# Full-height rotary matmul in attention scores, one round-robin burst for the in-chunk kernels of a block, and a planner class for 64-column matmuls

## The chip, the cores and the metric

The kernel runs on one core of a Trainium2 chip. The metric is the device time of one execution in microseconds. PE is TensorE (PEld is its weight load), DVE is VectorE, ACT is ScalarE, POOL is GpSimd and SP is SyncE, which issues most DMAs.

## What is computed

The program is a trunk of two layers over 256 latent tokens and 256 context tokens of width 1024, in float32. Each layer does a half-step SwiGLU FFN, then two token mixers on one normed input, then a second half-step FFN. All are wrapped in RMS norms with modulation from a conditioning vector. The two parts of the mixer that matter here:

```python
def mla_attend(q_n, q_r, k_n, k_r, v):
    s = jnp.einsum('bqhd,bkhd->bhqk', q_n, k_n) + jnp.einsum('bqhr,bkr->bhqk', q_r, k_r)
    p = jax.nn.softmax(s.astype(jnp.float32) * MLA_SCALE, axis=-1).astype(v.dtype)
    return jnp.einsum('bhqk,bkhd->bqhd', p, v)
```

There are 8 heads; a score has a part over 128 channels (q_n, k_n) and a rotary part over 64 channels (q_r, k_r). The other mixer is a bidirectional diagonal state-space layer (S5) of 64 groups of 16 channels with 64 complex states each:

```python
    xs_c = s5_scan(uc, a_bar, b_bar, reverse, None)
    xs_x = s5_scan(ux, a_bar, b_bar, reverse, s_ctx)
    y_x = y_x + s5_readout(xs_x, c_mat).reshape(B, L, S5_WIDTH)
```

In the last layer only the latent tokens are needed after the mixer.

## The kernel before

**Numbers.** Most products take three matmuls: an operand is split into a rounded part (hi) and a rest (lo), and hi·hi, hi·lo and lo·hi are added in one bank. Weights stream from DRAM as 256 KB pieces (`raw`), which ACT and DVE split into `whi` and `wlo`.

**The planner.** Instructions are not issued in the order of the text. `Recorder` records them all, each with a key (the time on the main path at which it was recorded, plus a shift for work that stands aside), and `schedule` (line 379) then simulates the engines and emits a list order; so every instruction of the trace has the emitter's line, L576, and is told apart by its tiles. A PE instruction has a mode (line 340): 1 for a stationary operand of at most 32 columns, 2 for all others. When the ready instruction with the least key is of another mode than the engine's present one, the planner first looks for ready ones of the present mode whose keys lie up to `TILE_PULL` = 12000 ns later (line 342). It charges `TILE` = 90 ns for a change into mode 2 only (line 498). Tiles of 512 columns come from a pool of `SLOTS` = 71 (line 27), shared by weights, activations and temporaries.

**Attention** (line 1311). A score (line 1359) is five matmuls into one bank for a 128-row block of queries and 512 or 256 keys: three for the 128 channels, then two for the rotary part. The rotary queries of a head are stacked as `st`: 64 partitions hold their hi, the other 64 their lo. The rotary keys stand twice, on both halves of the 128 partitions, as `krh` and `krl`. The fourth matmul takes all 128 rows, `st` by `krh`; the fifth takes only the 64 rows with the hi part, by `krl` (tiles `lo,qs` in the trace). There are 48 scores: 32 in layer 0 (16 by 512 keys and 16 by 256) and 16 in layer 1 (by 512).

**S5 build** (line 1599). This is done once per layer, beside the FFN ahead of the mixer, as recorded steps with keys pushed back by 15000 ns (layer 0) or 10000 ns (layer 1). For each of 8 blocks DVE makes `bz` (stationary columns, 32 for a pair of directions and group; one lasting tile for all blocks) and four readout tables `P` of 512 columns (two halves of the groups by two directions). A callback three steps after a half's second table records `kernels` (line 1668): 8 matmuls of 32 stationary columns by 128 moving ones (tiles `P,c`), four into one 32-partition group of the bank `kp`, then four into the next, and then the DMAs that store the tables. So a block has 16 matmuls in two calls; the profiler records two for each, 32 of a block and 512 in all. Afterwards `kout` copies the bank and the next tables follow.

**S5 run** (line 1734). This runs beside the mixer. For a block, 32 matmuls with 64 stationary columns (`uc,m1l`, 64 records) give the inputs; DVE rotates and scans; the states `X` are read out with 64-column matmuls in layer 0 (`X,pl` and `uc,tt`, 96 records of a block) and with 32-column ones in layer 1 (`pl,X` and `tt,uc`). Results go to DRAM and come back (`ys`) for the GLU that follows the attention output product.

**Others with 32 columns** are the modulation products (`aw,c`: a round-robin over the four 32-partition groups of a bank, line 791) and the norms' column sums (`tri,c`, `sq,c`).

Of the kernel before, what the change touches and what calls it, by code (L numbers as in the profile page):

```python
# [9 lines left out]
F32 = mybir.dt.float32  # L10
# [12 lines left out]
LEAD = 6  # L23
# [3 lines left out]
SLOTS, HALVES, ROWS, TRIS = 71, 8, 8, 4  # L27
# [45 lines left out]
class View:  # L73
    """A part of an on-chip tile, as strides over [128 partitions, columns]."""
# [55 lines left out]
    def extent(self):  # L130
        """The first partition, the last, and the columns as bits."""
        p, c = divmod(self.offset(), self.root.cols)
        key = c, self.arr.shape[1:], self.arr.strides[1:]
        if key not in MASKS:
            at = np.array([c])
            for n, st in zip(*key[1:]):
                at = (at[:, None] + st * np.arange(n if st else 1)).reshape(-1)
            m = 0
            for x in at.tolist():
                m |= 1 << x  # L140
            MASKS[key] = m
        return p, p + self.arr.shape[0], MASKS[key]
# [14 lines left out]
class Root:  # L157
    """A tile: lasting, or one of a tag's buffers from its first write to its last use."""
# [18 lines left out]
class Scratch:  # L177
    """A part of a DRAM tensor, with what tells it from parts that other instructions use."""
# [41 lines left out]
class Recorder:  # L220
    """Records instructions, then issues them in the order of a list schedule.

    An instruction waits for those that it depends on and for its buffers; each engine takes the one that was
    recorded for the earliest time among those that can run.
    """
# [18 lines left out]
    # ---------------------------------------------------------------- tiles  # L244
# [14 lines left out]
    # ---------------------------------------------------------------- priorities  # L259
    @contextmanager  # L260
    def aside(self, late, pace=0.0, lazy=False):
        """Work beside the main path, as if recorded some time later, and by and by.

        Lazy work is for an engine's idle time, up to the time at which its result is needed.
        """
# [8 lines left out]
    # ---------------------------------------------------------------- recording  # L274
    def cost(self, eng, method, a, kw):
        """Time on the engine, in ns."""
# [26 lines left out]
    def record(self, engine, method, a, kw):  # L303
# [35 lines left out]
        elif engine.code == "PE":  # L339
            op.mode = 1 if a[1].shape[-1] <= 32 else 2  # L340
# [37 lines left out]
    # ---------------------------------------------------------------- schedule  # L378
    def schedule(self):
# [12 lines left out]
        n = 0  # L392
# [35 lines left out]
        while left:  # L428
# [8 lines left out]
            for e in engines:  # L437
# [59 lines left out]
                if op.mode not in (0, mode[e]):  # L497
                    extra = self.TABLE if e == "ACT" else self.TILE if op.mode == 2 else 0
# [46 lines left out]
    def lacks(self, op):  # L545
        """A tile that the instruction is the first to use and that has to wait for a buffer, if there is one.

        A tile gets a buffer only if all that is still to come, in the order of the recording, then fits as well.
        """
# [29 lines left out]
class Trunk:  # L579
# [24 lines left out]
    # ---------------------------------------------------------------- storage  # L604
# [21 lines left out]
    # ---------------------------------------------------------------- fillers  # L626
    def add_filler(self, gen, interval, delay=0.0, late=0, pace=0.0, lazy=False):
        """A generator whose steps are recorded at intervals, with the priority of a later time.

        With a pace the intervals are that many times VectorE's work in a step.  # L630
        """
# [21 lines left out]
    # ---------------------------------------------------------------- weights  # L653
# [8 lines left out]
    def wget(self):  # L662
        """Loads and splits the weights that come next."""
# [14 lines left out]
    # ---------------------------------------------------------------- matmuls  # L678
# [20 lines left out]
    # ---------------------------------------------------------------- norms  # L699
    def part(self, t, h):  # L700
        """Half h of the tokens of a tile: 0 the context, 1 the latent ones, which an x-only tile holds alone."""
# [10 lines left out]
    def stat(self, r, q, n=1):  # L712
        """Adds a block's column sums to n regions of the statistics bank: 4 quadrants by 64 tokens."""
# [5 lines left out]
    def rsqrt(self, v, plain=False, wide=True, times=1.0, mask=None):  # L719
        """times/sqrt of [quadrant, token] rows: as they are, and with the tokens of other quadrants as zeros."""  # L720
# [28 lines left out]
    def rstd(self, r, width, n=1):  # L749
        """1/rms of the sums of squares in n regions from r on."""  # L750
# [4 lines left out]
    def spread(self, p, rows):  # L755
        """Rows of 64 tokens, one of each quadrant, to [128, 256 tokens] on every partition."""
# [8 lines left out]
    def close(self, l, s, i, h, y, src, fast, last=False):  # L765
        """Statistics of half h of block i of a branch's output: sums of src^2, y^2 and x y for y = G src."""
# [21 lines left out]
    # ---------------------------------------------------------------- modulation  # L788
    ADA_AHEAD = 4

    def ada_gen(self, units):
        """One step: one [128, 512] piece of ada_w for the two conditioning vectors."""
# [45 lines left out]
    def ada_first(self):  # L838
        """One step: a quarter of the channels of the two units that the first norm needs."""
# [24 lines left out]
    def ada_rows(self, units):  # L864
        """The same on the vector engine: one step gives 128 channels from their rows of the transposed ada_w."""
# [59 lines left out]
    # ---------------------------------------------------------------- FFN  # L925
    def lead(self, nrm, evac):
        """The first LEAD output blocks of a phase by pairs, one half of the tokens after the other."""
# [29 lines left out]
    def ffn(self, l, f, nrm, nxt):  # L957
        """nrm gives the normed input; nxt(y) makes the Norm that takes the output."""
# [58 lines left out]
    def gate_half(self, g, n):  # L1017
        """Makes the gated block j of half h of the tokens from a bank with both of its products."""
# [7 lines left out]
    def ffn_last(self, l, nrm):  # L1026
        """The last branch: its output has the tokens on partitions, where the norm has one scale per partition."""
# [75 lines left out]
    # ---------------------------------------------------------------- mixer  # L1103
# [197 lines left out]
    def rope(self, t):  # L1301
        """Axial rotation of [128 = two heads of 64, 256 x tokens], in place."""
# [8 lines left out]
    def attention(self, l, xo, cq, ckv, krh, krl):  # L1311
# [47 lines left out]
        def score(p, qs, kv, j, c, nk):  # L1359
            (qh, ql), st = qs[0][j], qs[1][j]  # L1360
            kh, kl = kv[0][j]
            a = slice(0, 64) if j == 0 else slice(64, 128)
# [5 lines left out]
            nc.tensor.matmul(p, st[a, c], krl[a, ks], start=False, stop=True)  # L1368
# [72 lines left out]
    # ---------------------------------------------------------------- S5  # L1441
    def cmul(self, ore, oim, are, aim, bre, bim, tmp):
        """Complex product of equal-shaped views; tmp: two scratch views; outputs may not alias inputs."""
# [8 lines left out]
    def s5_tables(self, l):  # L1452
        """Per-state tables: 192 columns; 0..63 (pair, dir) with (g2, n) on partitions, 64..191 (dir, g) with n twice."""
# [70 lines left out]
        # decay over eight steps  # L1524
# [5 lines left out]
        # unit phases 8, 16, 32, .. steps  # L1530
# [28 lines left out]
        # powers of the transition: 0..7 in the stacked columns, 1..8 in the pair columns  # L1559
# [39 lines left out]
    def s5_build(self, l):  # L1599
        """Per layer: chunk matrices to DRAM. Tensor-engine parts follow their operands by some steps."""  # L1600
# [6 lines left out]
        bz = self.s5c["bz"]  # L1607
# [21 lines left out]
        # rotation tables over the chunks  # L1629
# [16 lines left out]
        for b in range(NB):  # L1646
            stg = self.stg[l][b]
            pa, pb, pc = nxt
            # stacked b_bar in 32-column blocks of a pair, zero elsewhere
# [15 lines left out]
            # readout matrices C a^t and the in-chunk kernels K_t  # L1665
            kp = self.acc()

            def kernels(PT, half, stg=stg, kp=kp):
                for j in (2 * half, 2 * half + 1):
                    for g in (2 * j, 2 * j + 1):  # L1670
                        for d in (1, 0):
# [541 lines left out]
```

## Time and profile before

| | |
|---|---|
| timed runs | 2319.03, 2319.44, 2321.52 us; median 2319.44 us |
| the profiled execution, span from the first to the last instruction | 2323.8 us |
| PE busy | 2275.3 us (98%), 15768 matmuls |
| DVE busy | 1870.1 us (80%) |
| ACT busy | 1029.1 us (44%) |
| DMA queues, share of 16 engines | 47.8% hardware, 9.1% software |
| mean granted TensorE clock | 0.991 |

The span is one execution and not one of the three timed ones. A time of a matmul in a row is from its start to its modelled end, and ends overlap the next ones; what a matmul costs the engine is therefore read from start to start. In a row such as `128*32 128x128` the first pair is rows by columns of the stationary operand, the second is partitions by moving columns.

### The profile page before, as it was taken

How to read it: one execution, taken by the hardware profiler on the slowest of the kernel's cores; microseconds unless marked ns; L12 is line 12 of the kernel's file. 1: busy time of each engine (PE TensorE's matmuls, PEld its weight loads, DVE VectorE, ACT ScalarE, POOL GpSimd, SP SyncE). 2: the span in 40 equal slices, each digit the busy share in tenths (PEclk: the TensorE clock that was granted, in tenths of full speed). 3: DMA queues.
4: the chain of work that ended last, by engine and by line, in shares of the span. 5: the costliest groups of instructions: out<-in, count | busy, mean ns of one | idle time of the engine just before them, and what ended most of it. 6: DMA issues, size and time to landing. Idle time of an engine off the chain costs nothing. (4 is left out here: it accounts for less than half of the span.)

```text
span 2323.8 us, 43733 instructions
## 1 busy us (share of the span) xinstructions
PE 2275.3 (98%) x15768; PEld 1947.8 (84%) x15768; DVE 1870.1 (80%) x4313; ACT 1029.1 (44%) x2050; POOL 300.6 (13%) x455
## 2 busy tenths in 40 slices
PE   8999999999999999999999999999999999998998
PEld 6887878887888888898888888888889898897997
DVE  4997788889889889699997899898557678877554
ACT  5332233653246644543222463333246446575452
POOL 0010111430100200200100131100004110312000
PEclk9999999999999999999999999999999999998999
DMA  9354556966874546243564645656445795673562
GB/s 318 97 162 147 170 186 202 350 194 197 295 256 148 162 147 226 69 123 111 163 197 125 206 148 161 206 191 227 155 137 161 244 299 174 174 258 120 178 195 88
DMA packets 237481, 428.06 MB, mean 184 GB/s; under 512 B 29488, under 2 KB 58032, under 8 KB 237264
## 3 DMA queue, kind: packets, MB, share of 16 engines
q1 hardware_dynamic: 213904, 350.79, 47.8%
q0 software_dynamic: 23360, 74.48, 9.1%
q8 instruction: 124, 2.03, 0.4%
q14 instruction: 93, 0.76, 0.1%
HBM read 366.56 MB, written 58.59 MB: 183 GB/s over the span
## 5 line engine op out<-in xcount | busy, mean ns | idle before, releaser
L576 PE MATMUL acc<-hhi,whi 128*128 128x256 f32 (+2 forms) x2112 | 717.1, 345 | 4.8 <-ACT hhi L576 4.1
L576 PE MATMUL acc<-hhi,wlo 128*128 128x256 f32 (+2 forms) x2112 | 707.6, 343 | 0.0
L576 PE MATMUL acc<-hlo,whi 128*128 128x256 f32 (+2 forms) x2112 | 699.9, 342 | 1.5 <-DVE hlo L576 1.5
L576 ACT ACTIVATE whi<-raw 128x512 fp32r<-128x512 f32 x802 | 476.0, 623 | 367.1 <-PE acc L576 157.8
L576 DVE TENSOR_TENSOR wlo<-raw,whi 128x512 fp32r<-128x512 f32 x802 | 529.6, 686 | 125.4 <-ACT whi L576 75.8
L576 PEld LDWEIGHTS acc<-hhi,whi 128*128 128x128 f32 (+1 forms) x2112 | 398.8, 190 | 56.9 <-ACT hhi L576 6.7
L576 PEld LDWEIGHTS acc<-hhi,wlo 128*128 128x128 f32 (+1 forms) x2112 | 398.9, 190 | 47.5 <-issue 0.6
L576 PEld LDWEIGHTS acc<-hlo,whi 128*128 128x128 f32 (+1 forms) x2112 | 390.3, 189 | 50.8 <-DVE hlo L576 2.8
L576 PE MATMUL acc<-hi,whi 128*128 128x512 f32 (+1 forms) x1144 | 392.4, 345 | 1.5 <-ACT hi L576 1.5
L576 PE MATMUL acc<-lo,whi 128*128 128x512 f32 (+1 forms) x1144 | 389.0, 341 | 0.0
L576 PE MATMUL acc<-hi,wlo 128*128 128x512 f32 (+1 forms) x1144 | 378.8, 343 | 0.6 <-DVE wlo L576 0.6
L576 PEld LDWEIGHTS acc<-hi,whi 128*128 128x128 f32 x1144 | 215.3, 189 | 32.4 <-issue 5.1
L576 PEld LDWEIGHTS acc<-hi,wlo 128*128 128x128 f32 x1144 | 214.3, 189 | 27.6 <-DVE wlo L576 1.8
L576 PEld LDWEIGHTS acc<-lo,whi 128*128 128x128 f32 x1144 | 215.6, 189 | 24.6 <-issue 0.3
L576 ACT ACTIVATE sg<-acc 128x512 f32<-128x512 f32 (+1 forms) x129 | 64.8, 503 | 252.2 <-PE acc L576 234.3
L576 ACT ACTIVATE hi<-sg 128x512 fp32r<-128x512 f32 (+1 forms) x113 | 60.4, 540 | 158.1 <-DVE sg L576 129.6
L576 DVE TENSOR_TENSOR sg<-sg,acc 128x512 f32<-128x512 f32 (+1 forms) x97 | 55.6, 574 | 90.4 <-ACT sg L576 63.4
L576 POOL TENSOR_TENSOR tri<-x,y 128x256 f32<-128x256 f32 x54 | 54.7, 1018 | 323.5 <-ACT y L576 296.1
L576 DVE CUSTOM_DVE_ANT_0 ar<-ar,crow,adab 128x512 f32<-128x512 f32 x104 | 77.6, 750 | 4.5 <-DMA ar<-in_ada_t_dram 4.5
L576 DVE TENSOR_TENSOR lo<-sg,hi 128x512 fp32r<-128x512 f32 (+1 forms) x113 | 66.0, 589 | 17.5 <-ACT hi L576 9.9
L576 DVE CUSTOM_DVE_ANT_0 ar<-ar,crow,ah 128x512 f32<-128x512 f32 x104 | 78.8, 758 | 1.5 <-DMA ar<-in_ada_t_dram 0.9
L576 POOL DMA_DIRECT2D stg<-P x64 | 34.8, 543 | 345.1 <-DVE P L576 345.1
(249 smaller groups left out, 3282.2 us busy)
## 6 DMA issues: line engine op xcount, KB each, us to landing
raw<-in_w_gu_dram SPq DMA_DIRECT2D x352, 256.0 KB, 3.2
ar<-in_ada_t_dram SPq DMA_DIRECT2D x208, 256.0 KB, 3.4
raw<-in_w_dn_dram SPq DMA_DIRECT2D x176, 256.0 KB, 3.2
raw<-in_w_sq_dram SPq DMA_DIRECT2D x128, 256.0 KB, 4.6
raw<-in_w_in_dram SPq DMA_DIRECT2D x112, 256.0 KB, 4.9
m1l<-stg SPq DMA_DIRECT2D x96, 256.0 KB, 5.0
aw<-in_ada_w_dram SPq DMA_DIRECT2D x80, 256.0 KB, 5.8
stg<-P POOLq DMA_DIRECT2D x64, 256.0 KB, 3.8
```

The source lines that it names most:

```text
L576: getattr(getattr(self.tc.nc, engine), method)(*[real(v) for v in a], **{k: real(v) for k, v in kw.items()})
```

## The change

Three edits to instructions, beside the removal of comments and docstrings, which changes none.

The fifth matmul of a score takes all 128 rows:

```diff
-            a = slice(0, 64) if j == 0 else slice(64, 128)
...
-            nc.tensor.matmul(p, st[a, c], krl[a, ks], start=False, stop=True)
+            nc.tensor.matmul(p, st[:, c], krl[:, ks], start=False, stop=True)
```

The 16 in-chunk matmuls of a block are recorded by one call, after the second half's tables, and go round the four 32-partition groups; the DMAs that store the tables keep their places; `bz` gets a second lasting tile, and the pool one tile less:

```diff
-SLOTS, HALVES, ROWS, TRIS = 71, 8, 8, 4
+SLOTS, HALVES, ROWS, TRIS = 70, 8, 8, 4
...
+            bz = self.s5c["bz"][b % 2]
...
-            def kernels(PT, half, stg=stg, kp=kp):
-                for j in (2 * half, 2 * half + 1):
-                    for g in (2 * j, 2 * j + 1):
-                        for d in (1, 0):
-                            o = 112 * (1 - d)
-                            nc.tensor.matmul(kp[32 * j:32 * j + 32, o:o + 128],
-                                             bz[:, d * 256 + g * 32:d * 256 + g * 32 + 32],
-                                             PT[d][:, (g % 4) * 128:(g % 4) * 128 + 128],
-                                             start=g % 2 == 0 and d == 1, stop=g % 2 == 1, skip_group_check=True)
+            def keep(PT, half, stg=stg):
                 for d in range(2):
                     o = 2048 + d * 1024 + half * 512
                     nc.gpsimd.dma_start(stg[:, o:o + 512], PT[d])
+
+            def kernels(PTS, kp=kp, bz=bz):
+                for i in range(2):
+                    for d in (1, 0):
+                        for j in range(4):
+                            g, o = 2 * j + i, 112 * (1 - d)
+                            nc.tensor.matmul(kp[32 * j:32 * j + 32, o:o + 128],
+                                             bz[:, d * 256 + g * 32:d * 256 + g * 32 + 32],
+                                             PTS[j // 2][d][:, (g % 4) * 128:(g % 4) * 128 + 128],
+                                             start=i == 0 and d == 1, stop=i == 1, skip_group_check=True)
...
                     if d == 1:
-                        later(3, lambda PT=PT, half=half, f=kernels: f(PT, half))
+                        PTS.append(PT)
+                        later(3, lambda PT=PT, half=half, f=keep: f(PT, half))
+                        if half == 1:
+                            later(3, lambda PTS=PTS, f=kernels: f(PTS))
...
-        nc.vector.memset(self.s5c["bz"], 0.0)
+        for t in self.s5c["bz"]:
+            nc.vector.memset(t, 0.0)
```

The planner gets a third mode, for float32 stationary operands of 33 to 64 columns, and charges every change of mode:

```diff
-            op.mode = 1 if a[1].shape[-1] <= 32 else 2
+            op.mode = 1 if a[1].shape[-1] <= 32 else 3 if a[1].shape[-1] <= 64 and a[1].dt == F32 else 2
...
-                    extra = self.TABLE if e == "ACT" else self.TILE if op.mode == 2 else 0
+                    extra = self.TABLE if e == "ACT" else self.TILE
```

The S5 matmuls with 64 stationary columns (`uc,m1l`, and in layer 0 `X,pl` and `uc,tt`) are of the third mode; the rotary key projection, also 64 columns wide, is not float32 and stays in mode 2.

## Rows read from the trace of the kernel before

**Rows 1.** The page: span, and busy time (share) by engine.
```profile
span 2323.8 us, 43733 instructions
PE 2275.3 (98%) x15768; PEld 1947.8 (84%) x15768; DVE 1870.1 (80%) x4313; ACT 1029.1 (44%) x2050; POOL 300.6 (13%) x455
```
**Rows 2.** Windows view, both build stretches: us, busy by engine, PEclk, DMA share, GB/s.
```profile
232.00:440.00 208.00, 207.60 (x1449) 170.14 (x1448) 172.31 (x306) 72.62 (x136) 38.72 (x70) 1.00 0.65 220
1394.00:1560.00 166.00, 164.77 (x832) 137.92 (x831) 151.72 (x321) 58.44 (x104) 15.83 (x28) 1.00 0.57 183
```
**Rows 3.** Waits of PE: us in total, times, longest.
```profile
PE acc L576 <- DVE wlo L576: 0.6, 2, 0.4
```
**Rows 4.** Groups of PE by form: busy us, mean ns, idle before.
```profile
L576 PE MATMUL acc<-P,c 128*32 128x128 f32 x512 | 48.4, 276 | 1.1 <-DVE c L576 1.1
L576 PE MATMUL acc<-aw,c 128*32 128x128 f32 x640 | 35.2, 296 | 10.3 <-ACT c L576 6.6 <-DMA aw<-in_ada_w_dram 3.6
L576 PE MATMUL acc<-uc,m1l 128*64 128x64 f32 x1024 | 35.0, 224 | 0.0
L576 PE MATMUL acc<-lo,qs 64*128 64x512 f32 x32 | 15.9, 497 | 0.0
```
**Rows 5.** Timeline of PE in attention, layer 0: start us, us, instruction.
```profile
681.57 0.39 PE L576 MATMUL acc<-hi,lo 128*128 128x512 f32 x1
681.80 0.40 PE L576 MATMUL acc<-hi,qs 128*128 128x512 f32 x1
682.13 0.50 PE L576 MATMUL acc<-lo,qs 64*128 64x512 f32 x1
682.56 0.50 PE L576 MATMUL acc<-hi,hi 128*128 128x512 f32 x1
682.90 0.40 PE L576 MATMUL acc<-lo,hi 128*128 128x512 f32 x1
...
684.58 0.29 PE L576 MATMUL acc<-hi,qs 128*128 128x256 f32 x1
684.80 0.38 PE L576 MATMUL acc<-lo,qs 64*128 64x256 f32 x1
685.11 0.39 PE L576 MATMUL acc<-hi,hi 128*128 128x256 f32 x1
```
**Rows 6.** Timeline of PE in the S5 build, layer 0.
```profile
288.53 2.46 PE L576 MATMUL acc<-P,c 128*32 128x128 f32 x32
290.93 0.66 PE L576 MATMUL acc<-ident,mt 128*128 128x128 f32 x4
...
338.35 1.53 PE L576 MATMUL acc<-P,c 128*32 128x128 f32 x16
339.80 0.50 PE L576 MATMUL acc<-hhi,whi 128*128 128x512 f32 x1
```
**Rows 7.** Timeline of PE in the first FFN: modulation products.
```profile
44.62 1.08 PE L576 MATMUL acc<-aw,c 128*32 128x128 f32 x32
45.63 0.74 PE L576 MATMUL acc<-hlo,whi 128*128 128x256 f32 x4
```
**Rows 8.** Timeline of PE in the S5 runs, layers 0 and 1.
```profile
592.76 2.09 PE L576 MATMUL acc<-uc,m1l 128*64 128x64 f32 x64
594.77 0.50 PE L576 MATMUL acc<-hhi,whi 128*128 128x512 f32 x1
...
1947.86 0.68 PE L576 MATMUL acc<-uc,m1l 128*64 128x64 f32 x14
1948.47 0.62 PE L576 MATMUL acc<-hi,hi 128*128 128x512 f32 x2
```
**Rows 9.** Timeline of DVE at the end of layer 1's S5 run.
```profile
2019.08 2.03 DVE L576 TENSOR_TENSOR X<-t,t 64x128 f32<-64x128 f32 x8
```
**Rows 10.** Timeline of PE at the end of layer 1's S5 run.
```profile
2032.66 0.30 PE L576 MATMUL acc<-tt,uc 128*32 128x128 f32 x1
2041.33 0.39 PE L576 MATMUL acc<-hi,whi 128*128 128x256 f32 x1 [1.48 <-ACT hi L576]
```

More of the change, by code (lines that the diff above doesn't have):

```diff
@@ L1606, in s5_build @@
         g1, g2 = self.s5c["g1"], self.s5c["g2"]
-        bz = self.s5c["bz"]
         queue = []
@@ L1684, in kout @@
                 later(1, lambda: nc.gpsimd.dma_start(self.k_dram[l][b], kb))
+            PTS = []
             for half in range(2):
@@ L1943, in run @@
         self.s5t = self.gate = None
-        self.s5c = dict(r8=self.const([128, 64]), g1=self.const([128, 128]), g2=self.const([128, 128]), bz=self.const([128, 512]))
+        self.s5c = dict(r8=self.const([128, 64]), g1=self.const([128, 128]), g2=self.const([128, 128]), bz=[self.const([128, 512]) for _ in range(2)])
         self.ada = self.ada_gen([(l, m) for l in range(L) for m in range(9) if (l, m) not in ADA_ROWS + [(0, 0), (0, 1)]])
```

## The prediction

> **What bounds the kernel now.** I read the page first: PE is busy for 2275.3 of 2323.8 us, so at most 48.5 us of the span are not TensorE's, and the next engine, DVE, is at 80% [rows 1]. Then the windows of the two stretches in which the S5 build runs: PE is busy for 207.60 of 208 us and for 164.77 of 166 us at a granted clock of 1.00, that is at 2.4 GHz, while DVE has 35.7 and 14.3 us free [rows 2]. Then what PE waited for: the split of a weight by DVE, the last step of the weight stream, ended 0.6 us of PE's idle time in the whole run [rows 3]. So a microsecond taken out of PE's queue should come off the span nearly in full, as long as nothing else becomes late. The rest is read from the groups by form and from PE's timeline, start to start, because busy PE is not PE at its peak: stalls between matmuls of different tile shapes hide in busy time.
>
> **The change part by part.**
>
> *Scores.* In a score by 512 keys the matmul ahead of the 64-row one starts at 681.80 us, the 64-row one at 682.13, the next at 682.56 and the one after that at 682.90 [rows 5]. Those are steps of 0.33, 0.43 and 0.34 us, where the tail of an undisturbed stream of 512 columns steps by 0.23 (681.57 to 681.80). Three steps of 0.23 are 0.69; they took 1.10; the lone 64-row matmul costs 0.41 us more than a full one would, 0.10 ahead of it, 0.20 behind it and 0.11 one further. By 256 keys the first two steps are 0.22 and 0.31 us [rows 5] against 0.12 each, which is 0.29, and the third is again 0.10 too long, so 0.39. The mean length of the 64-row form, 497 ns, against some 400 ns for the 128-row forms beside it, says the same of its own part [rows 4]. A full matmul streams the same columns and adds no instruction, weight load or tile. 48 scores by 0.39 are 18.7 us; three of them stand next to another change of shape, which stays, so I take 18.2. Bounds: 48 x 0.29 = 13.9 if the third step's excess has another cause, 48 x 0.41 = 19.7.
>
> The Trainium skill, in "TensorEngine Tiling (Array Packing)", section "When to Use Tiling", recommends two row tiles where the contracted dimension is 64, and its section "Theoretical Speedup" gives up to 2x for it. By that rule the old form was the better one and this edit would be worth nothing; the sum would then be 18 us smaller. The row disagrees: the tiled matmul stands alone between full ones, and has no partner in the other row tile.
>
> *In-chunk kernels.* Today a block's 32 records run as two bursts of 16, as at 338.35: from its start to the next full matmul's it takes 1.45 us [rows 6]. With 0.10 us of entry and 0.11 behind it, as at the score, a half costs 1.66 and a block 3.3 us. Where both halves fell together, at 288.53, the body took 2.40 [rows 6], 2.6 in all. The group's row says 48.4 us for 16 blocks, 3.0 each [rows 4]; I count 32 bursts with this group in the timeline. The modulation products have the same shape and go round the four groups: 32 records take 1.01 us from start to start [rows 7], 1.22 with entry and tail. The whole group shows it too: 55 ns of busy time for each record (35.2 us / 640) against 95 ns (48.4 / 512) [rows 4]. So a block goes from 3.0-3.3 to 1.2 us, and 16 blocks from 48.4 to 19.5: 28.9 us. The first two start matmuls of a burst can run before the second half's tables are ready, which would cut off a small piece (0.4 us); others will join a modulation or norm burst and save their entry. I take 28. Bounds: 16 x (3.3 - 2.6) = 11 if going round the groups brings no overlap and only the halves are joined; 31 if all is whole and a third of the blocks share an entry.
>
> The stores of the tables keep their step and their POOL queue. The bank's copy stands where it stood. A first half's two tables stay in the pool some steps longer, and the pool has one tile less: this could delay weights. PE lost 0.6 us to late weight splits so far [rows 3], so I price it at 1 us; below, zero; above, 6 us, ten times that. The second memset lies at the very start, where DVE has no inputs yet: nothing. The second `bz` tile takes a DVE wait away, on an engine that is not the bound: nothing.
>
> *Third mode.* A whole input burst of 64 records takes 2.01 us and a piece of 14 takes 0.61 [rows 8]. That is 0.028 us for a record and 0.22 fixed; with entry (0.10) and tail (0.11) a piece costs 0.43 us extra. In the timeline three input bursts of layer 1 lie in 4, 3 and 2 pieces and three readouts of layer 0 in 3, 4 and 3: 13 pieces too many, 5.6 us. Seven times in layer 0 a readout and the next input burst are some ten matmuls apart and could merge: 3 us. The input group holds 35.0 us of busy time in all [rows 4]; 8.6 us is the most that is at stake in both. Some pieces come from data that isn't ready, which a class doesn't cure: I take 5, with bounds of 0 and 8.6 for this effect alone. The charge for changing into mode 1 changes only the planner's own clock, and is counted with the noise of a new order.
>
> The class has a price: a 64-column burst may now be put off by up to 12 us of main-path keys, as 32-column ones already are. In layer 0 the S5 run ends over 100 us before its result is used: hidden. In layer 1 it is nearly late now. The last block's states are written at 2019.08 to 2021.11 us [rows 9], its readout starts at 2032.66, and PE stood for 1.48 us before 2041.33 for what follows from it [rows 10]. So the last input burst can come 2032.66 - 2021.11 = 11.6 us later before the readout moves, just about the 12 us. But layer 1's attention, in which PE arrives 16 x 0.4 = 6 us sooner, runs into this same end, whose DMAs don't get faster. I give back 4 us there (bounds 0 and 12).
>
> *Sum.* -18.2 - 28 - 5 + 1 + 4 = -46.2 us. Against the profiled execution that is 2323.8 - 46.2 = 2277.6 us of span. The median of the timed runs is 4.4 us below that execution, and the edits are the same for both: 2319.4 - 46.2 = 2273.2, and I say 2274.
>
> **The rivals.**
>
> 1. *The gain is taken back by the suppliers.* PE is faster by 14 us in each build, and DVE or the weight stream doesn't follow. For it: in 1394-1560 DVE has only 14.3 us free of 166. Against it: much of DVE's work there is paced to fill idle time, and PE has no idle time to show that it waits. If one layer's share is lost: 2274 + 14 = 2288.
> 2. *The bursts don't overlap or don't stay whole*, that is, the change doesn't do what it says: the kernels' gain is the 11 us of the lower bound, and the class brings nothing. 2319.4 - 18.2 - 11 + 5 = 2295. Against it: the modulation products have the same shape, bank and order, and do overlap [rows 7].
> 3. *The 64-row matmul was no loss* (the rule above): 2274 + 18 = 2292. For it there is only that the steps around it could be long for another reason; 45 scores with the same excess speak against it.
> 4. *The S5 chain of layer 1 carries its delays along: slower.* If each block's input burst is put off by 12 us and the next block's waits for it (for the pool's tiles), 8 blocks add up to 96 us, less the 11.6 us of slack: PE would stand for 84 us more at the GLU, 2274 + 84 = 2358. The point from which it is slower than before is 7.2 us carried over per block ((46 + 11.6) / 8). Against it: the input burst of a block needs its own loads and not the block before, and the planner gives the 64-column class to PE as soon as nothing of mode 2 is ready, which is often in the attention.
>
> **How the numbers follow.** The forecast as summed has 0.70, with a range of its own of 2260 to 2288 from the bounds (all upper ends: 19.7 + 31 + 8.6 = 59, 2260; scores and kernels a little short and 10 us given back: 2288). Rival 1 has 0.12, rival 2 has 0.09, rival 3 has 0.04 and rival 4 has 0.05. The range of 2258 to 2297 holds the first three cases. About 0.2% (4.6 us) is what a measurement of this kernel can tell from no change. Only rival 4 gives slower (0.04, with 0.02 left for a carried delay that just cancels the gain); the others are all faster by over 20 us: 0.94.
>
> **What would show it.** The scores' group `lo,qs` with 64 rows is gone, one with 128 rows is there with some 400 and 285 ns, and the steps around it are 0.23 or 0.12 us. `P,c` falls from 48.4 to about 20 us busy in about 16 to 20 bursts, and a whole burst's body takes 1.0 us. `uc,m1l` stands in pieces of 64, often right behind a readout. PE's busy time falls by about 47 us and its idle time stays near 48. The forecast is wrong if PE's idle time grows by more than 10 us (rivals 1 and 4, told apart by where: in the builds, or around 2000 us), if a burst of 32 still takes 2.4 us (rival 2), or if full-height scores still show steps of 0.4 us (rival 3).

## The result and the profile after

The changed kernel takes 2301.66 us (median of 4 runs, 2300.88 to 2302.47); the kernel before, run beside it, takes 2320.02 (2319.03 to 2321.52). The ratio is 0.9918, 95% interval 0.9904 to 0.9932. It is faster by 18.4 us where the forecast was 46: the sign was right, the size was not, and the time lies above the range of 2258 to 2297 us.

The first profiled execution of the kernel before was an ordinary one except in one place: a second profile of the same kernel spans 2319.6 us, and as good as all of the 4.2 us between the two arise between 1994 and 2121 us. Stretches below are compared with the second profile.

The page of the changed kernel, its first two lines; the second answers to [rows 1]:

```profile
span 2299.7 us, 43776 instructions
PE 2236.4 (97%) x15768; PEld 1926.3 (84%) x15768; DVE 1870.4 (81%) x4314; ACT 1034.4 (45%) x2050; POOL 297.0 (13%) x455
```

PE's busy time fell by 38.9 us, not far from the 47 of the forecast. But what PE isn't busy grew from 48.5 us (44.2 in the second profile) to 63.3. The groups of PE by form, changed kernel, answering to [rows 4]:

```profile
L576 PE MATMUL acc<-uc,m1l 128*64 128x64 f32 x1024 | 32.9, 223 | 0.0
L576 PE MATMUL acc<-P,c 128*32 128x128 f32 x512 | 24.3, 283 | 0.0
L576 PE MATMUL acc<-lo,qs 128*128 128x512 f32 x32 | 13.2, 412 | 0.0
L576 PE MATMUL acc<-lo,qs 128*128 128x256 f32 x16 | 4.6, 289 | 0.0
```

Each row moved as the change said: `P,c` from 48.4 to 24.3 us, `lo,qs` of 512 columns from 497 to 412 ns. PE's timeline in layer 0's attention (start, us, instruction), answering to [rows 5], has no long step left around a score's fifth matmul:

```profile
674.20 0.39 PE L576 MATMUL acc<-hi,lo 128*128 128x512 f32 x1
674.42 0.39 PE L576 MATMUL acc<-hi,qs 128*128 128x512 f32 x1
674.65 0.40 PE L576 MATMUL acc<-lo,qs 128*128 128x512 f32 x1
674.89 0.28 PE L576 MATMUL acc<-hi,hi 128*128 128x256 f32 x1
675.01 0.27 PE L576 MATMUL acc<-lo,hi 128*128 128x256 f32 x1
```

From start to start 0.22, 0.23, 0.24 and, by 256 keys, 0.12 us. In the run with this edit alone (e1, below) the very steps that took 1.10 before are three of 0.23 (starts at 681.30, 681.53, 681.76 and 681.99 us). And a whole burst of in-chunk kernels, answering to [rows 6], takes 0.99 us from its start to the next matmul's, where 2.40 stood:

```profile
287.82 1.06 PE L576 MATMUL acc<-P,c 128*32 128x128 f32 x32
288.81 0.66 PE L576 MATMUL acc<-ident,mt 128*128 128x128 f32 x4
```

So where is the rest? I cut both executions at the same instructions (matmuls that spread a norm's rows) into six stretches: layer 0's first FFN, its mixer, its second FFN with layer 1's first, layer 1's norm and projections, its attention and what follows up to the last norm, the last FFN. The windows view gives for each its bounds, its length, and the busy time of PE, PEld, DVE, ACT and POOL, then the granted clock as a share of 2.4 GHz, the DMA share and GB/s. First the second profile of the kernel before, then the changed kernel:

```profile
0.00:474.81 474.81, 461.49 (x3206) 378.50 (x3206) 387.52 (x872) 190.24 (x366) 64.42 (x111) 0.99 0.61 201
474.81:983.06 508.25, 504.10 (x3799) 419.87 (x3799) 431.09 (x1005) 244.62 (x501) 70.26 (x111) 1.00 0.60 192
983.06:1748.21 765.15, 759.48 (x4091) 643.74 (x4089) 653.08 (x1515) 286.95 (x537) 76.70 (x118) 1.00 0.51 165
1748.21:1854.18 105.97, 105.40 (x953) 93.17 (x954) 73.48 (x209) 57.88 (x124) 30.77 (x39) 1.00 0.62 200
1854.18:2115.87 261.69, 250.80 (x2383) 230.35 (x2382) 217.20 (x502) 158.32 (x338) 54.95 (x71) 0.99 0.71 223
2115.87:2311.28 195.41, 194.19 (x1342) 181.20 (x1342) 104.35 (x202) 89.98 (x183) 4.51 (x6) 0.98 0.45 142
```

```profile
0.00:469.25 469.25, 450.87 (x3208) 365.90 (x3208) 388.45 (x875) 192.30 (x368) 62.98 (x111) 0.99 0.60 203
469.25:967.76 498.51, 489.26 (x3798) 419.11 (x3798) 430.72 (x1006) 245.49 (x502) 71.63 (x112) 0.99 0.61 196
967.76:1730.03 762.27, 754.13 (x4091) 638.54 (x4090) 654.14 (x1515) 289.71 (x538) 75.17 (x117) 0.99 0.51 167
1730.03:1835.83 105.80, 103.34 (x960) 91.37 (x958) 68.65 (x196) 55.50 (x120) 27.70 (x39) 1.00 0.56 182
1835.83:2096.58 260.75, 245.24 (x2380) 230.82 (x2378) 220.48 (x512) 160.23 (x342) 55.07 (x71) 0.98 0.73 228
2096.58:2291.43 194.85, 193.57 (x1342) 180.60 (x1342) 104.18 (x202) 90.49 (x183) 4.45 (x6) 0.98 0.44 144
```

Length against PE's busy time, stretch by stretch: -5.6 against -10.6, -9.7 against -14.8, -2.9 against -5.4, -0.2 against -2.1, -0.9 against -5.6. In each of these five PE works less and then stands for a good part of what it saved. The waits of PE that grew (us in all, times, longest), changed kernel:

```profile
PE acc L576 <- DVE sp L576: 8.4, 5, 4.6
PE acc L576 <- DVE hlo L576: 4.8, 7, 2.9
PE acc L576 <- DVE lo L576: 4.4, 7, 1.5
PE acc L576 <- ACT pr L576: 4.2, 2, 4.0
PE acc L576 <- issue: 3.0, 1, 3.0
```

### The profile page after: what moved, and what is told of

Its sections match the earlier page's. It is cut to its first block, busy times and chain, and to the rows that moved or that the text cites. A ratio compares the mean times of both kernels' runs of the same rounds, so it can differ in the third digit from the quotient of the medians.

```text
span 2299.7 us, 43776 instructions
## 1 busy us (share of the span) xinstructions
PE 2236.4 (97%) x15768; PEld 1926.3 (84%) x15768; DVE 1870.4 (81%) x4314; ACT 1034.4 (45%) x2050; POOL 297.0 (13%) x455
## 4 chain that ended last, share of the span: by engine, by line
PE 75%; DVE 8%; DMA 3%; issue 1%; ACT 1%; POOL 0%; DVEq 0%; SPq 0%; ACTq 0%; POOLq 0%
PE acc L576 74%; DVE rs L576 1%; DVE t L576 1%; DVE wlo L576 1%; DMA aw<-in_ada_w_dram 1%; PE misc L576 1%; DVE lo L576 1%; DVE w L576 1%; DMA ar<-in_ada_t_dram 0%; DMA m1l<-stg 0%; DMA raw<-in_w_in_dram 0%; DVE po L576 0%; DVE hlo L576 0%; DVE X L576 0%; DVE sp L576 0%
## 5 line engine op out<-in xcount | busy, mean ns | idle before, releaser
L576 PE MATMUL acc<-hi,wlo 128*128 128x512 f32 (+1 forms) x1144 | 384.2, 343 | 1.0 <-DVE wlo L576 1.0
```

The lines of the kernel that those rows point to most:

```text
L576: getattr(getattr(self.tc.nc, engine), method)(*[real(v) for v in a], **{k: real(v) for k, v in kw.items()})
```

## The experiments

All times are medians; a ratio is against the kernel before, run beside it on the same chip. An interval reaches 2 to 5 us to either side.

**One part at a time.** The score's edit alone (e1), the in-chunk kernels with the second `bz` and the pool of 70 alone (e2), the planner's third mode with its charge alone (e3), and e1 with e2 (e4, the changed kernel without the planner's edits). Their diffs are the three of the change.

> Only the score edit; the planner emits the same order on every engine as before, so nothing but the length of PE's steps changes. Theory S (PE's saving is real, but other engines and DMAs take a part of it back as idle time of PE): PE busy falls by 17 to 19 us, of which 12 us in layer 0 come through in full and the 6 us of layer 1 come through by half or less: 2302 to 2308 us against 2320. Rival R (what was lost in the changed kernel was lost by the new order that planner class and pool size bring, not by suppliers): all 18 us come through, 2302 or less. If the 64-row matmul was no loss: 2320.

> Only the in-chunk kernels (one round-robin burst of a block, second bz tile, pool of 70). PE busy should fall by 24 to 28 us in either theory. Theory S: half of it comes back as idle time in the stretches with a high DMA share (end of the first FFN, start of the mixers): 2304 to 2312 us. Rival R: a new order costs up to 10 us anywhere, at places that have no high DMA share; the time is then anywhere from 2295 to 2315, and the idle time is not near 400 to 460 us.

> Only the planner's edits (third mode and the charge for every change). PE's busy time falls by 4 to 8 us for fewer changes of shape. Theory S: 2313 to 2318 us. Rival R: idle time that the class brings (input bursts and readouts put off) is as large as the saving or larger: 2318 to 2328 us.

> Score and kernels edits without the planner's edits. Theory S: 2299 to 2306 us, the class adds some 4 us of gain on top. Rival R: better than the changed kernel, 2285 to 2298 us, since the class is what costs.

| | us | ratio, interval | against before |
|---|---|---|---|
| e1, score | 2305.91 | 0.9938 (0.9926 to 0.9951) | -14.0 |
| e2, kernels | 2313.02 | 0.9961 (0.9948 to 0.9975) | -6.9 |
| e3, class | 2327.21 | 1.0027 (1.0018 to 1.0037) | +7.3 |
| e4, score and kernels | 2293.78 | 0.9886 (0.9873 to 0.9900) | -26.1 |

The expectations had two theories, S (the suppliers take a part back) and R (a new order costs it). e1 lies in the range of S, e2, e3 and e4 in that of R: the class, and not the suppliers alone, holds the time up. The score gives 14.0 us. The kernels give 12.1 on top of it (e4 against e1), 6.9 alone; most of what lies between these two values is in the stretch of layer 1's attention, 265.88 us in e2 and 261.69 in the kernel before, and why is open. The class is a loss: +7.3 alone, and 2301.66 - 2293.78 = +7.9 on top of the rest. In e1 PE's busy time is 2258.1 us against 2275.3 [rows 1], 17.2 less; the mixer of layer 0 keeps 2.7 us of it as new idle time, and layer 1's attention, where theory S expected the loss, keeps none (6.3 us shorter for 5.7 of PE). In e4 the two FFN stretches in which a build runs tell different things (windows view):

```profile
0.00:463.96 463.96, 449.58 (x3208) 366.96 (x3209) 386.12 (x872) 190.47 (x367) 62.39 (x110) 1.00 0.62 206
962.69:1728.49 765.80, 752.95 (x4088) 636.12 (x4087) 653.45 (x1517) 288.28 (x536) 78.16 (x117) 0.99 0.51 165
```

Layer 0's build: PE does 11.9 us less, the stretch is 10.9 us shorter. Layer 1's: PE does 6.5 us less, and the stretch is 0.65 us *longer*. The kernels' gain of layer 1 is lost inside it.

**Is it the round-robin or the joining?** e5 is e4 with the joined call going one column group after another.

```diff
-                for i in range(2):
-                    for d in (1, 0):
-                        for j in range(4):
+                for j in range(4):
+                    for i in range(2):
+                        for d in (1, 0):
```

> As e4 (score and kernels, no planner edits), but the joined call goes through the four column groups one after the other, as before the change. If the saving of the kernels comes from going round the groups: a burst's body is 2.4 us again in place of 1.0, PE busy rises by 16 x 1.4 = 22 us over e4, and the time by half of that or more: 2305 to 2316 us. If it comes from joining two bursts into one (one entry less): PE busy rises by under 8 us, 2294 to 2300 us.

2303.38 us, 0.9927 (0.9912 to 0.9941): 9.6 slower than e4, between the two ranges that were expected. Groups and timeline of PE in e5:

```profile
L576 PE MATMUL acc<-P,c 128*32 128x128 f32 x512 | 43.1, 276 | 0.0
```

```profile
293.26 2.44 PE L576 MATMUL acc<-P,c 128*32 128x128 f32 x32
295.63 0.33 PE L576 MATMUL acc<-ident,mt 128*128 128x128 f32 x1
```

The same 32 matmuls take 2.37 us instead of 0.99: it is the order. Joining alone brought the row from 48.4 to 43.1, the order another 19.2 (e4: 23.9). PE's whole busy time rises by 12.7 us only (2238.8 to 2251.5), so other groups were longer in e4, and 9.6 are in the time. By stretch, e4 to e5: +5.6 in layer 0's FFN, +2.5 in its mixer, in which no in-chunk kernel runs, and in layer 1's 765.80 to 765.76, nothing, although PE is busy 7.5 us longer there. In layer 1 the round-robin as built buys idle time only.

**Where it is lost.** The phase change at the start of layer 1's first FFN. The windows view of 32 us there, in the kernel before, and of the 32 us that begin 7.9 us ahead of the last matmuls of the norm (`sp,c`, at 1382.51 us):

```profile
1364.00:1396.00 32.00, 30.17 (x242) 27.99 (x242) 30.37 (x86) 18.36 (x39) 13.66 (x20) 0.95 0.29 96
1374.60:1406.60 32.00, 30.77 (x246) 29.64 (x246) 30.73 (x81) 18.03 (x38) 7.77 (x11) 0.97 0.33 104
```

The same place in e5, counted from the same matmuls (at 1373.17 us):

```profile
1365.00:1397.00 32.00, 30.59 (x240) 29.02 (x241) 30.89 (x83) 19.47 (x41) 8.69 (x10) 1.00 0.34 108
```

And the same place in e4 (the matmuls are at 1359.89 us), in four pieces, with PE's timeline there:

```profile
1352.00:1368.00 16.00, 10.42 (x68) 9.00 (x68) 16.00 (x47) 7.79 (x16) 4.14 (x5) 0.94 0.09 34
1368.00:1372.00 4.00, 0.00 (x0) 0.00 (x0) 4.00 (x10) 0.38 (x1) 0.00 (x0) 0.50 0.00 0
1372.00:1376.20 4.20, 4.13 (x38) 3.64 (x39) 4.00 (x10) 0.93 (x3) 1.10 (x2) 0.50 0.28 71
1376.20:1384.00 7.80, 7.24 (x60) 7.04 (x59) 7.02 (x17) 4.32 (x11) 3.70 (x5) 1.00 0.44 147
```

```profile
1365.97 1.64 PE L576 MATMUL acc<-hlo,whi 128*128 128x256 f32 x6 [2.04 <-DVE hlo L576]
1372.07 1.92 PE L576 MATMUL acc<-P,c 128*32 128x128 f32 x28 [4.46 <-DVE P L576]
1373.92 0.58 PE L576 MATMUL acc<-hlo,whi 128*128 128x256 f32 x1
1374.30 0.42 PE L576 MATMUL acc<-hhi,wlo 128*128 128x256 f32 x1
1374.51 0.41 PE L576 MATMUL acc<-hlo,whi 128*128 128x256 f32 x1
```

At the same matmuls DVE is busy 30.73 of 32 us before and PE 30.77, in e5 30.89 and 30.59. In e4 DVE is busy 31.02 and PE 21.79. PE, early, has come up against DVE, which works through the norm's halves, the build's tables and the modulation rows, from 1352 to 1372 us without a gap. PE waits 2.04 us for `hlo` and 4.46 for `P`, and from the end of the first of these waits the clock is granted at half speed, 1.2 GHz (0.50 from 1366.0 to 1376.2 us): steps of 256 columns take 0.21 us instead of 0.12. Up to the first `sp,c` of this norm e4 is 6.1 us faster than e5 (366.8 us from the start of the stretch against 372.9); at the end of the stretch nothing of that is left.

**Which work on DVE?** Four ways to take it off this place, all on e4. e8 puts the kernels' callback three steps later. e9 leaves out the second half of layer 1's modulation rows on DVE, 66 us of it, and e10 does the same on e5. e13 starts a build's steps closer together, e14 puts layer 1's build back by 30000 ns of keys instead of 10000.

```diff
-                            later(3, lambda PTS=PTS, f=kernels: f(PTS))
+                            later(6, lambda PTS=PTS, f=kernels: f(PTS))
...
-            later(5, kout)
+            later(8, kout)
```

> e4, with the joined kernels recorded six steps after the second half's tables in place of three (and the copy of their bank eight in place of five). If the joined burst stops PE because it waits for the second half's tables (5.6 us of PE waits for DVE P in e4, 4.5 of them at the head of layer 1's second FFN stretch): that wait is gone and the time is 2286 to 2291 us. If something else would hold PE there anyway: 2292 to 2296 us.

```diff
-                    for i in range(2):
+                    for i in range(2 - l):
...
```

> e4 with DVE relieved: of the modulation rows of layer 1 that DVE multiplies and sums, the second half of each row is left out (72 units of work by 2 or 1 instructions of 0.75 us less, all loads kept), so layer 1's modulation is computed from half of its inputs. If DVE at the phase change (1330 to 1384 us in e4, back to back) is what takes the kernels' saving back in layer 1: PE's idle time there falls from 12 to 4 us or less, and the time is 2280 to 2287 us. If PE would wait there for something else: 2291 to 2296 us.

> e5 (joined, column groups one after the other) with the same work left out of DVE. The kernels cost PE 18.8 us more here than in e9. If DVE takes the saving back, then with DVE relieved more of the difference shows: 14 to 19 us slower than e9, where it was 9.6 with DVE loaded. If not, the difference stays at 8 to 11 us.

```diff
-PACE_A, PACE_B = 1.6, 2.5
+PACE_A, PACE_B = 1.6, 2.1
```

> e4 with layer 1's S5 build paced at 2.1 times its DVE work in place of 2.5, so that more of it lies ahead of the phase change at 1330 us. If DVE's load at the phase change takes the kernels' saving of layer 1 back: PE's idle time in the 60 us around it falls from 11 us to 5 or less, and the time is 2285 to 2290 us. If the same idle time turns up elsewhere: 2292 to 2297 us.

```diff
-LATE_A, LATE_B, LATE_C, URGENT = 0, 15000, 10000, 1500
+LATE_A, LATE_B, LATE_C, URGENT = 0, 15000, 30000, 1500
```

> e4 with layer 1's S5 build given keys 30000 ns late in place of 10000, so that at the phase change the norm's and the FFN's own DVE work goes ahead of the tables. If DVE's order at the phase change is the cause: idle there 5 us or less and 2285 to 2290 us, unless the build is then late for layer 1's mixer, which would show as PE idle after 1740 us and 2295 us or more. If neither: 2292 to 2297 us.

| | us | ratio, interval | against e4 |
|---|---|---|---|
| e8, kernels later | 2295.97 | 0.9896 (0.9881 to 0.9911) | +2.2 |
| e9, fewer rows, round-robin | 2287.17 | 0.9863 (0.9849 to 0.9878) | -6.6 |
| e10, fewer rows, group after group | 2295.40 | 0.9901 (0.9886 to 0.9916) | +1.6 |
| e13, build steps closer | 2299.91 | 0.9911 (0.9896 to 0.9926) | +6.1 |
| e14, layer 1's build later | 2286.13 | 0.9849 (0.9833 to 0.9866) | -7.7 |

The last column subtracts medians; by the ratios it would read +2.3, -5.3, +3.5, +5.8 and -8.6, because the runs of the kernel before beside them differ by up to 3 us. In e8 the wait for `P` stays, 4.0 us at the same place, so it isn't the callback's own step that is too early; DVE is behind with everything. Less work on DVE (e9, just above its first range) or its later placing (e14) helps; work pressed closer (e13, above both of its ranges) hurts: the wait for `P` falls to 1.2 us, but PE waits 6.9 us for `wlo`. In e14 the phase change reads (windows view, the two middle pieces):

```profile
1368.00:1372.00 4.00, 3.35 (x28) 3.15 (x27) 4.00 (x12) 2.68 (x6) 1.17 (x2) 1.00 0.54 197
1372.00:1376.20 4.20, 4.20 (x37) 4.20 (x36) 4.10 (x12) 2.92 (x7) 0.00 (x0) 1.00 0.56 184
```

PE works, and the clock stays at 1.00. The stretch of both FFNs falls from 765.80 to 759.08 us, and PE's idle time in it from 12.9 to 8.0.

But e10 speaks against it: with DVE relieved the order of the groups should have been worth more than e4 against e5, and it was 8.2 us instead of 9.6, in the range for "if not". So I asked the same of e14: e17 is e14 with e5's order.

> e14 (layer 1's build 30000 ns late) with the joined call going through the column groups one after the other, as in e5. PE has 18 to 20 us more to do. If the early build is what kept layer 1's half of the kernels' saving from showing: 13 to 19 us slower than e14, 2299 to 2305 us, and in 964 to 1830 us at least 5 us slower. If something else in layer 1 holds it: 6 to 10 us slower, 2292 to 2296 us, nearly all of it in the first FFN of layer 0.

2299.54 us, 0.9913 (0.9893 to 0.9933): 13.4 slower than e14 (14.8 by the ratios), where it was 9.6 without the later build. That is at the low end of what the theory expects, and with intervals of 3 to 5 us the times alone don't tell 13.4 from 9.6. The stretches say more, though each is read from one execution. The one with layer 1's build takes 764.02 us against 759.08: the round-robin is worth 4.9 us there now, and was worth nothing. Together with the waits of e4 for `hlo` and `P`, which e5 and e14 all but lack at this place, this shows that DVE took back most of layer 1's gain at the phase change. That DVE is all that holds layer 1 is not shown: PE is busy 7.8 us longer there in e17, so some 3 of its 8 us are still swallowed, and between e9 and e10 the order is worth 6.7 us in the stretch of the FFNs (751.3 and 758.0 us), of which 4.7 are lost again in the norm and projections behind it. What takes the rest stays open.

**Which half of the class hurts?** e6 is e4 with the third mode alone, e7 with the charge alone, e11 the changed kernel with the mode's delay cut from 12000 to 2000 ns.

```diff
+        if op.mode == 3 and engine.code == "PE":
+            op.pull = 2000
```

> e4 and the third mode, without the charge for changes into modes 1 and 3. If putting 64-column bursts off is what costs (merged bursts of 128 records in layer 1's attention, softmax late, PE idle for 4 us there): 2299 to 2304 us, the PE wait for ACT pr near the end of layer 1's attention is there. If the charge costs: 2292 to 2296 us.

> e4 and the charge for every change of mode, without the third mode. If the mode costs: 2290 to 2297 us, as e4, with no late softmax. If the charge costs (a new order with a slower planner clock): 2299 to 2304 us.

> The changed kernel, with 64-column bursts put off by up to 2000 ns of keys in place of 12000. If the long delay is what makes the class cost 8 us (layer 1's softmax late behind merged bursts): 2290 to 2296 us, and no wait of 4 us for ACT pr. If the class costs by its grouping at any delay, or by the new order: 2299 to 2304 us.

| | us | ratio, interval | against e4 |
|---|---|---|---|
| e6, mode alone | 2302.33 | 0.9919 (0.9902 to 0.9935) | +8.5 |
| e7, charge alone | 2296.94 | 0.9893 (0.9879 to 0.9908) | +3.2 |
| e11, both, short delay | 2294.14 | 0.9894 (0.9878 to 0.9911) | +0.4 |

By the ratios the last column would read +7.7, +1.6 and +1.9. It is the mode, and most of its cost goes with the delay (e11). In e6 layer 0's mixer is 4.5 us shorter than in e4 and the stretch of layer 1's attention 12.0 us longer (255.71 to 267.76): PE stands 8.4 us longer there, 4.0 of it for the softmax's `pr` and 2.7 for `yt`, the S5 run's own output, and is busy 3.7 us longer at a granted clock of 0.97 in place of 0.99. In the changed kernel the same stretch is 5.0 us longer than in e4. PE's timeline there shows the largest of the waits that e4 doesn't have:

```profile
1943.47 3.95 PE L576 MATMUL acc<-uc,m1l 128*64 128x64 f32 x128
1947.35 0.50 PE L576 MATMUL acc<-lo,hi 128*128 128x512 f32 x1
...
1951.16 0.33 PE L576 MATMUL acc<-ident,pr 128*128 128x128 f32 x1 [0.36 <-ACT qr L576]
1955.52 0.70 PE L576 MATMUL acc<-qr,rot 128*128 128x256 f32 x2 [4.03 <-ACT pr L576]
1955.99 0.64 PE L576 MATMUL acc<-hi,hi 128*128 128x512 f32 x1
1956.43 0.63 PE L576 MATMUL acc<-lo,hi 128*128 128x512 f32 x1
```

The input bursts of two blocks have merged, 128 records, and lie in the middle of a score. The rest of the score, and so its softmax, comes 3.9 us later; PE runs through what else is ready and then stands for 4.03 us for the probabilities (`pr`). After that the clock is at half speed again: 0.44 and 0.42 us for 512 columns instead of 0.23. The windows view of the standstill and of what follows, changed kernel, and of the second of the two in e11:

```profile
1951.00:1955.50 4.50, 0.33 (x1) 0.14 (x1) 4.36 (x15) 0.89 (x3) 0.00 (x0) 1.00 0.96 341
1955.50:1959.20 3.70, 3.68 (x13) 2.92 (x14) 3.02 (x10) 0.91 (x2) 0.00 (x0) 0.59 0.42 153
```

```profile
1955.50:1959.20 3.70, 3.70 (x33) 3.66 (x33) 3.36 (x9) 2.87 (x6) 0.57 (x1) 1.00 0.74 182
```

In e11 a whole burst still stands in this part, but one block's only (64 records, 2.08 us), and PE doesn't stop here. Behind the next one, at 1967.25 us, it does: 3.1 us in three waits for `pr`, and then the clock is at half speed too:

```profile
1972.40:1979.20 6.80, 5.33 (x23) 5.03 (x24) 5.98 (x17) 5.17 (x12) 0.00 (x0) 0.50 0.21 54
```

And in e3 a merged burst of 127 records (3.94 us from 1966.28 us) is followed by only 1.3 us of waits for `pr`. So a long burst doesn't always stop PE this long, and a short one can. Of the 7.5 us between the changed kernel and e11, 2.9 lie in layer 1's attention, 2.1 in layer 0's mixer and the rest in small parts elsewhere. That the delay costs is shown by e11; that the late softmax is the way is shown for the one wait of 4.03 us and argued for the rest. The charge moves the order in layer 0's first FFN, where e7 and the changed kernel are 4.9 and 5.3 us longer than e4; what in the new order costs that, and why e11 has the same there and gains it elsewhere, was not followed up. The gap of 3.0 us that the waits put down to "issue" lies at 541 us, between layer 0's readouts; it appears with the class only (e3 has one of 3.1 us, e11 none), and its cause stays open too.

**The small edits.** e15 is e4 with one `bz` and a pool of 71; e16 is the kernel before with a pool of 70.

```diff
-SLOTS, HALVES, ROWS, TRIS = 71, 8, 8, 4
+SLOTS, HALVES, ROWS, TRIS = 70, 8, 8, 4
```

> e4 with one bz tile and the pool of 71, as before the change. If the smaller pool costs: faster than e4 by 2 us or more. If the second bz tile is worth something: slower by 2 us or more. I expect 2292 to 2297 us, no difference.

> The kernel before with a pool of 70 and nothing else, which gives a new order of all engines from PE's row 266 on with the same work. If a new order by itself moves the time (rival R): 2310 or 2330, over 4 us from 2320. If not: 2317 to 2322 us, PE busy as before.

e15 takes 2294.71 us, 0.9889 (0.9874 to 0.9904), as e4 does. e16 takes 2323.09, 1.0009 (1.0000 to 1.0019), 2.5 us more than the kernel before beside it and between its two ranges. On e4 neither the second `bz` nor the pool matters, and a new order by itself moves the time by 2 or 3 us: differences of that size between two orders are not explained here.

**The kernel before once more** (e12) gave the second profile.

> The kernel before, profiled again. If the first profiled execution was slow by itself around 2000 us, where e1, with the same order, has 6 us less: this one has a span near 2318 us and idle time of PE between the last score and the last norm of 9 to 11 us in place of 14. If not: the same 2323 us and 14 us, and e1's gain there is its own.

One run of 2321.35 us, span 2319.6. In the stretch from layer 1's attention to the last norm PE stands for 10.9 us in place of 14.2, so the first profile was slow there by itself, and e1's gain there is not its own.

**The best version.** e14 beats both kernels: 2286.13 us, 0.9849 (0.9833 to 0.9866). e18 adds the class with the short delay to it.

> e14 with the third mode, its charge, and 64-column bursts put off by up to 2000 ns (as in e11). If the class at a short delay is worth what its merged bursts save (e6 gained 4.5 us in layer 0's mixer): 2280 to 2284 us. If it only changes the order: 2284 to 2292 us, as e11 stood to e4.

2288.15 us, 0.9857 (0.9841 to 0.9874): no better, in its second range. The version to keep is the score and the kernels, none of the planner's edits, and layer 1's build 20000 ns later.

## Why the prediction was right in sign and wrong in size

The forecast was -46.2 us. By experiment the parts are -14.0 (e1), -12.1 (e4 against e1) and +7.9 (changed kernel against e4), together -18.2. Of the 28 us of error, 4 are the scores', 15 the kernels' with the pool, 9 the class's with its give-back. The split goes by the order in which the parts are added; alone, the kernels give 6.9.

*Scores: right.* PE's busy time fell by 17.2 us for the 18.2 of the sum, by the three steps that were named, and 14.0 reached the end. Rival 3 falls: the rule of the Trainium skill ("TensorEngine Tiling (Array Packing)", "When to Use Tiling") that two row tiles suit a contraction over 64 does not pay for a tiled matmul alone between full ones, here by 14.0 us. The same page says under "Key Properties" that a change of mode drains TensorE, without a price; e1 fits that, at some 0.4 us a score (1.10 us for three steps that now take 0.69).

*In-chunk kernels: right on the burst, too large on PE, wrong on the time. This is the step that failed most.* A whole burst is 1.0 us as read from the modulation products, and rival 2 falls; e5 shows what it would have looked like. On PE the sum was too large: `P,c` lost 24.1 us where 28 was taken, since not every burst stays whole (in e4 one block's runs as 24, 6 and 2 records, at 284.07, 286.11 and 287.60 us), and PE's whole busy time fell by only 19.3 from e1 to e4. The sum also took 19.5 us counted from start to start away from 48.4 us of busy time, in which ends overlap. The large loss is the step "a microsecond taken out of PE's queue should come off the span nearly in full". It held in layer 0 (10.9 us shorter) and failed in layer 1, which is 0.5 us shorter over both its stretches in e4, for a `P,c` that takes 12.1 us less and a PE that is busy 8.0 us less there. That is rival 1, "DVE or the weight stream doesn't follow", with its price of 14 near the 15 that are missing and its chance of 0.12 too small. The argument against it was the wrong one: the stretch read for layer 1 was 1394 to 1560 us, where DVE has 14.3 us free [rows 2], and most of the phase change, in which DVE was free for 1.6 of 32, lies ahead of it. And [rows 3] was one row of a list: in the same list DVE, with `sp`, `rs`, `tri`, `hlo`, `c`, `lo` and `wlo`, ends 17.0 us of PE's idle time in the kernel before. That PE had little idle time showed only that the two engines arrived together, not which would be late if one got faster.

*Third mode: its bursts about right, wrong on the time.* `uc,m1l` fell by 2.1 us [rows 4], and start to start the 64-column bursts, with the entries, take about 7 us less than in e4 by estimate, for the 5 that was taken; but PE's whole busy time is only 2.4 us below that of e4. The price was looked for in the wrong place. The prediction saw a late input burst as a delay of its own chain, by the states and the readout at 2032 us, and gave back 4 us there; rival 4 had the same chain. What happened in the changed kernel is the reverse: the burst, merged and long, stands in front of others, and the softmax pays, 4.0 of the 5.0 us by which layer 1's attention is longer than in e4. (In e6 the S5 run's own output is late as well, 2.7 us of its 12.0.) With a delay of 12000 ns two blocks' inputs go together; with 2000 ns they don't (e11). The other large part, 5.3 us in layer 0's first FFN, comes with the new order that the charge brings (4.9 in e7); the prediction counted it as noise, and its cause is open.

*Pool +1:* no effect found on e4 (e15), and 2.5 us on the kernel before (e16), no more than a new order moves; neither confirms the term. *Tail give-back +4:* the wrong place, as said.

*What would show it.* The list asked whether idle time grows by more than 10 us, and where. It grew by 14.8 (19.1 against the second profile), so the mark was the right one, but by 2 to 5 us in each of five stretches, since the class's new order had moved idle time about too. The place alone didn't tell the rivals apart in the changed kernel; the runs with one part each did.

## What to carry to other kernels

Where the bound engine and the next one are both near full in some stretch, the gain of the first ends at the second's free time there, so read the windows at each phase change and not only in the steady part: with 30.2 and 30.4 of 32 us busy there was room for less than 2 us. A planner rule that merges small bursts saves their entries, but the merged burst is a block that others wait behind: keep its delay short, and measure whether it pays. Here 12000 ns cost 7.9 us and 2000 ns next to nothing (e11), but no version with the class beat the one without. And after a gain on one engine, move the work that it now runs into: layer 1's build put back by 20000 ns was worth another 7.7 us.

## What the runs showed of the hardware

A standstill of PE can cost more than its length. In e4 PE stood for 2.04 us up to 1365.97 us, and the granted clock was 0.50, 1.2 GHz, from 1366.0 to 1376.2; PE worked for 1.64 us, stood for another 4.46, and then a burst of 28 records took 1.85 us where a whole one of 32 takes 0.98 in the same run (at 290.58), and nine steps of 256 columns took 0.21 us instead of 0.12, some 0.8 us more. After 4.03 us of waiting in the changed kernel five steps of 512 took 0.43 instead of 0.23, 1.0 us more. Not every standstill does this: after one of 2.95 us, up to 544.05 us in the changed kernel, the clock stayed at 1.00.

The order of small matmuls matters by a factor of more than two: 32 records with 32 stationary columns take 0.98 us round the four column groups (e4) and 2.37 group after group (e5), with nothing else changed in the text of the kernel.
